# Last group of feed-forward tiles: four tiles with low halves from DVE, evictions first, and a last norm multiplied from PSUM

## The chip, the cores and the metric

The kernel runs on one core of a Trainium2 chip. TensorE (PE) multiplies matrices, VectorE (DVE) and ScalarE (ACT) work on tiles in SBUF and in PSUM, GpSimd (POOL) works on tiles in SBUF and issues some transfers, SyncE (SP) issues the others, and 16 DMA engines move the data. The metric is the time of one execution in microseconds (us); lower is better. The time of a kernel is the median of several runs.

## The reference

One layer of a streaming encoder over 1024 prompt and 64 sample tokens, width 1024, in float32. Three recurrent mixers follow one input projection and are joined by an output projection; then come the feed-forward part and the final norm, which are what matters here:

```python
x = x + jnp.einsum('ble,ed->bld', mix, P['w_out'][l])
xn2 = rmsnorm(x, P['norm_ffn'][l])
hid = (jax.nn.silu(jnp.einsum('bld,df->blf', xn2, P['w_ffn_gate'][l]))
       * jnp.einsum('bld,df->blf', xn2, P['w_ffn_up'][l]))
x = x + jnp.einsum('blf,fd->bld', hid, P['w_ffn_down'][l])
...
y = rmsnorm(x, P['norm_final'])
```

The hidden width is 2816, which is 22 tiles of 128.

## The kernel before

Everything lies transposed: the 128 partitions hold features, the free axis tokens. The tokens form three token groups (`GROUPS`) of 384, 384 and 320. The float32 products are made of three passes in a reduced format (fp32r): each operand is split into a high half (a rounded copy) and a low half (the rest), and `dense` (L128) adds high x high, low input x high weight and, last, high input x low weight in one PSUM tile.

`weights_part` (L110) brings a weight tile of up to four 128 x 128 blocks (256 KB). SP loads it to `raw` (three buffers), ACT casts it to the high half `whi` (L117; five buffers). The low half `wlo` (five buffers) is made in one of two ways. With `add=True`, ACT writes the negated high half (L119) and a DMA that POOL issues reads the weights again and adds them to it (L120). With `add=False`, DVE subtracts the high half from `raw` (L122). A product over five blocks needs two such tiles, one of 128x512 and one of 128x128.

The feed-forward part takes the 22 hidden tiles in five groups (`ffg`, L1292). In each, gate and up products are made for every hidden tile and the three token groups (PSUM tags `pg`, `pu`). Then `down` (L1322) makes the down products: for each of eight output tiles `dm`, a product over the group's hidden tiles into PSUM (`ps_d`, tag `pd`, two buffers), which DVE adds to the residual `x1` (L1326), called the eviction here. In the first four groups a weight tile serves three token groups. In the last one the token groups are the outer loop: 3 x 8 products, each with weights of its own. These 24 products are called the last stage here.

In the last stage each eviction is followed on ACT by a square (L204, L207) and a scaling by the norm's gain (L1338), and on DVE by adding the squares to `sacc` (L210). The final norm of a token group is made while the next one is multiplied: behind the third product (`dm == 2`) PE sums `sacc` over the partitions (`row_sums`, L212, tag `pt`), and DVE computes the inverse root in a chain of small steps and writes two diagonal tiles `dg` (`inv_rms`, L228). Behind the fifth product PE spreads them over the partitions (`spread`, L244), DVE copies the result to SBUF, and `write_y` (L1282) multiplies the eight tiles of `x1` by it and sends them out.

A scheduler sets each engine's order beforehand; an engine works through its list strictly in order. Instructions under `tc.high_priority(offset=WPRIO)` (WPRIO is 400) are taken as if written 400 places earlier; weights and the steps behind the gate and up products have it, the evictions of `down` don't. PE's order is that of the program text (`in_order`, L70).

Of the kernel before, what the change touches and what calls it, by code (L numbers as in the profile page):

```python
# [14 lines left out]
OP = mybir.AluOpType  # L15
# [17 lines left out]
WPRIO = 400  # L33
# [25 lines left out]
def trunk(ctx: ExitStack, tc: tile.TileContext, I: dict, O: list):  # L59
    nc = tc.nc  # L60
    V, A, G, PE = nc.vector, nc.scalar, nc.gpsimd, nc.tensor
    tt = V.tensor_tensor
# [7 lines left out]
    def in_order(ins):  # L70
        if last_pe[0] is not None:
            tc.add_manual_dep(ins, last_pe[0].name, NOSYNC, reason="tensor engine order")
        last_pe[0] = ins

    def mm(out, lhsT, rhs, start=True, stop=True, **kw):
        in_order(PE.matmul(out, lhsT, rhs, start=start, stop=stop, **kw).ins)  # L76
# [48 lines left out]
    def weights(src, add=True):  # L125
        return [p for h0 in range(0, src.shape[1], 4) for p in weights_part(src, h0, add=add)[0]]
# [25 lines left out]
    x1, x2, mhl, sums = {}, {}, {}, {}  # L152
# [91 lines left out]
    def spread(gi, diags, pst, out):  # L244
        T = GROUPS[gi]["T"]
        pn = pst()
        for i, dg in enumerate(diags):
            mm(pn[:, :T], ones_r, dg.rearrange("p i t -> p (i t)")[:, :T], start=(i == 0), stop=(i == 1))
        V.tensor_copy(out[:, :T], pn[:, :T])

    def x2prep(gi, pool, tiles):
        T = GROUPS[gi]["T"]
# [1020 lines left out]
    for i, _ in enumerate(outproj(2, p2, p2, 4, ps_d)):  # L1273
        if i == 1:
            diags = inv_rms(1, row_sums(1, [sums[1]], ps_t))
# [5 lines left out]

    def write_y(gi, diags, out):  # L1282
        T, t0 = GROUPS[gi]["T"], GROUPS[gi]["tok"]
        spread(gi, diags, ps_t, out)
        pieces = (0, 1, 2, 4, 6, 8) if gi == 2 else (0, 2, 4, 6, 8)
        for k0, k1 in zip(pieces, pieces[1:]):
            for k in range(k0, k1):
                xo = x1[gi][:, k, :T]
                (tt if k % 4 != 3 else G.tensor_tensor)(xo, xo, out[:, :T], op=OP.mult)  # L1289
            nc.sync.dma_start(y_out[:, k0:k1, t0:t0 + T], x1[gi][:, k0:k1, :T])  # L1290

    ffg = [4, 4, 4, 5, 5]  # L1292
    f0 = 0
    for fi, nf in enumerate(ffg):
        hid = []
        for m in range(f0, f0 + nf):
# [5 lines left out]
            for gi, grp in enumerate(GROUPS):  # L1302
                T, t0 = grp["T"], grp["tok"]
# [3 lines left out]
                if m == 0 and gi == 0:  # L1307
                    diags = inv_rms(2, row_sums(2, [sums[2]], ps_t))
# [11 lines left out]
        last = fi == len(ffg) - 1  # L1320

        def down(parts, gi, dm):  # L1322
            T, t0 = GROUPS[gi]["T"], GROUPS[gi]["tok"]
            o = ps_d()
            dense(o[:, :T], parts, lambda k: (hid[k][0][:, t0:t0 + T], hid[k][1][:, t0:t0 + T]))
            tt(x1[gi][:, dm, :T], o[:, :T], x1[gi][:, dm, :T], op=OP.add)  # L1326

        for gi in range(3) if last else (None,):
            if last:
                sacc = p2.tile([128, TMAX], F32, tag="sacc", name="sacc", bufs=2)  # L1330
            for dm in range(NK):
                parts = weights(I["w_down"][dm][:, f0:f0 + nf, :])
                for g in (gi,) if last else range(3):
                    down(parts, g, dm)
                if last:
                    xo = x1[gi][:, dm, :GROUPS[gi]["T"]]
                    part = square_sum(sacc, xo, dm, p2, 4, gi == 2 and dm == NK - 1)
                    A.activation(xo, xo, AF.Copy, scale=col("ny", dm))  # L1338
                if dm == 2 and gi:
                    pend = inv_rms(gi - 1, row_sums(gi - 1, [prev], ps_t))  # L1340
                if dm == 4 and gi:
                    write_y(gi - 1, pend, prev)
            prev = sacc if last else None
# [79 lines left out]
```

## Time and profile before

| what | value |
|---|---|
| median of 3 runs | 1402.28 us (1399.97 to 1403.4) |
| profiled execution | 1400.07 us, span 1398.3 us |
| PE busy | 1310.6 us (94%) |
| ACT busy | 651.2 us (47%) |
| DVE busy | 613.5 us (44%) |
| POOL busy | 333.8 us (24%) |
| mean DMA rate | 127 GB/s |

The page of the profile divides the span into 40 equal slices. PE is at 9 tenths (90% or more) from about the 17th to the 37th slice and falls to 8, 8 and 5 in the last three; ACT, POOL and the DMA engines, which have little to do in the middle, rise at the same place. Shares of the whole span say nothing about that end, so the stretches must be read one by one: for each, which engine is busy, what the others wait for, and at which clock PE ran.

### The profile page before, as it was taken

The numbers are of one execution on the slowest core, as the hardware profiler recorded it, in microseconds if no ns is written. First come the engines' busy times: TensorE is split into PE (matmuls) and PEld (weight loads), VectorE is DVE, ScalarE is ACT, GpSimd is POOL, SyncE is SP. The second block draws the span as 40 slices with busy tenths as digits, with TensorE's granted clock in tenths as the row PEclk, the third lists the DMA queues.
The fourth block names the chain that finished last, engine by engine and source line by source line (L and its number), as shares of the span: only waits on it lengthen the run. The fifth ranks groups of instructions, "written<-read, shape, count | busy, mean of one in ns | idle before, by whom it ended". The sixth has DMA issues, their size and how long they took to land.

```text
span 1398.3 us, 21341 instructions
## 1 busy us (share of the span) xinstructions
PE 1310.6 (94%) x7872; PEld 1253.7 (90%) x7872; DVE 613.5 (44%) x1685; ACT 651.2 (47%) x1300; POOL 333.8 (24%) x405
## 2 busy tenths in 40 slices
PE   7878998989988998999999999999999999999885
PEld 7877897878877897999999999999999999999874
DVE  9876798857667577711221121112211121111255
ACT  7766757768875454532213231323132322332763
POOL 2334344434342000110201010101011121111453
PEclk8998999999997999999999999999999999999997
DMA  9967687677692343452525352435344355352996
GB/s 288 290 135 189 130 179 158 152 157 178 137 227 60 115 151 123 108 112 62 122 58 117 65 121 61 102 79 113 69 86 96 63 99 111 75 107 57 174 219 153
DMA packets 114184, 178.22 MB, mean 127 GB/s; under 512 B 13744, under 2 KB 40896, under 8 KB 114080
## 3 DMA queue, kind: packets, MB, share of 16 engines
q0 software_dynamic: 41696, 69.65, 30.8%
q1 hardware_dynamic: 72384, 107.21, 24.3%
q8 instruction: 62, 1.02, 0.3%
q14 instruction: 42, 0.34, 0.1%
HBM read 169.10 MB, written 7.12 MB: 126 GB/s over the span
## 4 chain that ended last, share of the span: by engine, by line
issue 54%; PE 16%; POOL 13%; DVE 10%; DMA 3%; ACT 3%; SPq 0%; POOLq 0%; DVEq 0%; ACTq 0%
POOL wlo L120 12%; PE mm L76 9%; PE mx L76 6%; DMA wlo<-in_w_in_dram 1%; PE pd L76 1%; DMA raw<-in_w_in_dram 1%; ACT wlo L119 0%; DVE x L1289 0%; ACT L138 0%; ACT whi L117 0%; DMA wlo<-in_w_down_dram 0%; DVE xl L325 0%; DVE hist L667 0%; DVE xc L522 0%; SPq L897 0%
## 5 line engine op out<-in xcount | busy, mean ns | idle before, releaser
L117 ACT CAST whi<-raw 128x512 fp32r<-128x512 f32 x336 | 195.2, 585 | 261.0 <-PE pd L76 162.1
L1317 DVE TENSOR_TENSOR sil<-pu,sil 128x384 f32<-128x384 f32 (+1 forms) x66 | 35.3, 536 | 404.5 <-PE pu L76 404.5
L76 PE MATMUL mm<-xh,whi 128*128 128x384 f32 (+1 forms) x480 | 168.4, 358 | 16.8 <-ACT whi L117 8.9
L76 PE MATMUL pd<-hh,whi 128*128 128x384 f32 (+1 forms) x528 | 173.2, 332 | 4.1 <-DVE x L1326 4.1
L76 PE MATMUL pd<-hl,whi 128*128 128x384 f32 (+1 forms) x528 | 172.3, 330 | 0.0
L76 PE MATMUL pg<-x2h,whi 128*128 128x384 f32 (+1 forms) x528 | 170.3, 327 | 0.6 <-ACT x2h L258 0.6
L76 PE MATMUL pg<-x2l,whi 128*128 128x384 f32 (+1 forms) x528 | 170.4, 327 | 0.3 <-DVE x2l L259 0.3
L76 PE MATMUL pu<-x2h,whi 128*128 128x384 f32 (+1 forms) x528 | 170.0, 327 | 0.0
L76 PE MATMUL pu<-x2l,whi 128*128 128x384 f32 (+1 forms) x528 | 169.9, 326 | 0.0
L119 ACT ACTIVATE wlo<-whi 128x512 fp32r<-128x512 f32 (+1 forms) x288 | 164.1, 590 | 4.1 <-issue 1.2
L76 PE MATMUL mm<-xl,whi 128*128 128x384 f32 (+1 forms) x480 | 159.8, 340 | 5.0 <-DVE xl L325 5.0
L120 POOL DMA_DIRECT2D wlo<-in_w_in_dram x112 | 100.2, 980 | 212.6 <-ACT wlo L119 178.9
L120 POOL DMA_DIRECT2D wlo<-in_w_gate_dram x44 | 42.0, 954 | 453.9 <-ACT wlo L119 370.0
L1326 DVE TENSOR_TENSOR x<-pd,x 128x384 f32<-128x384 f32 (+1 forms) x120 | 64.0, 535 | 161.4 <-PE pd L76 161.3
L120 POOL DMA_DIRECT2D wlo<-in_w_down_dram x88 | 77.6, 968 | 216.6 <-ACT wlo L119 175.5
L1318 ACT CAST hh<-sil 128x384 fp32r<-128x384 f32 (+1 forms) x66 | 32.7, 496 | 186.9 <-DVE sil L1317 186.9
L76 PE MATMUL pd<-hh,wlo 128*128 128x384 f32 (+1 forms) x528 | 109.9, 333 | 9.8 <-DMA wlo<-in_w_down_dram 9.7
L76 PEld LDWEIGHTS mm<-xh,whi 128*128 128x128 f32 x480 | 95.2, 199 | 24.5 <-ACT whi L117 9.5
L76 PEld LDWEIGHTS pd<-hh,whi 128*128 128x128 f32 x528 | 100.7, 191 | 4.6 <-ACT whi L117 2.3
L76 PEld LDWEIGHTS pd<-hh,wlo 128*128 128x128 f32 x528 | 90.6, 191 | 14.4 <-DMA wlo<-in_w_down_dram 14.0
L76 PEld LDWEIGHTS mm<-xl,whi 128*128 128x128 f32 x480 | 95.0, 199 | 9.1 <-DVE xl L325 6.3
L76 PE MATMUL mm<-xh,wlo 128*128 128x384 f32 (+1 forms) x480 | 93.4, 333 | 8.4 <-DMA wlo<-in_w_in_dram 8.3
(428 smaller groups left out, 2596.7 us busy)
## 6 DMA issues: line engine op xcount, KB each, us to landing
raw<-in_w_in_dram SPq DMA_DIRECT2D x112, 256.0 KB, 4.5
wlo<-in_w_in_dram POOLq DMA_DIRECT2D x112, 256.0 KB, 5.8
raw<-in_w_down_dram SPq DMA_DIRECT2D x56, 256.0 KB, 4.5
wlo<-in_w_down_dram POOLq DMA_DIRECT2D x56, 256.0 KB, 5.2
raw<-in_w_out_dram SPq DMA_DIRECT2D x48, 256.0 KB, 3.0
raw<-in_w_gate_dram SPq DMA_DIRECT2D x44, 256.0 KB, 2.7
raw<-in_w_up_dram SPq DMA_DIRECT2D x44, 256.0 KB, 5.3
wlo<-in_w_gate_dram POOLq DMA_DIRECT2D x44, 256.0 KB, 4.6
```

The costliest lines, as they stand in the source:

```text
L76: in_order(PE.matmul(out, lhsT, rhs, start=start, stop=stop, **kw).ins)
L117: ins = A.copy(hi[:, :n, :], raw[:, :n, :]).ins
L119: A.activation(lo[:, :n, :], hi[:, :n, :].bitcast(F32), AF.Copy, scale=-1.0)
L120: G.dma_start(lo[:, :n, :], src[:, h0:h0 + n, :], accum_op=OP.add)
L1317: tt(s_[:, :T], pu[:, :T], s_[:, :T], op=OP.mult)
L1318: A.copy(hh[:, t0:t0 + T], s_[:, :T])
L1326: tt(x1[gi][:, dm, :T], o[:, :T], x1[gi][:, dm, :T], op=OP.add)
```

## The change

- The groups of hidden tiles are 5, 5, 4, 4, 4 instead of 4, 4, 4, 5, 5.
- In the last group the low halves of the down weights come from DVE (`add=False`) instead of from an accumulating DMA.
- The evictions of `down`, and the row sums and inverse roots of the first two token groups, have high priority.
- `write_y` makes all eight multiplies of a token group on DVE; two of them were on POOL.
- For the last token group the multiplies read the spread factor from PSUM, without the copy.

```diff
@@ spread
+        if out is None:
+            return pn
         V.tensor_copy(out[:, :T], pn[:, :T])
+        return out
@@ write_y
-        spread(gi, diags, ps_t, out)
+        out = spread(gi, diags, ps_t, None if gi == 2 else out)
...
-                (tt if k % 4 != 3 else G.tensor_tensor)(xo, xo, out[:, :T], op=OP.mult)
+                tt(xo, xo, out[:, :T], op=OP.mult)
...
-    ffg = [4, 4, 4, 5, 5]
+    ffg = [5, 5, 4, 4, 4]
@@ down
-            tt(x1[gi][:, dm, :T], o[:, :T], x1[gi][:, dm, :T], op=OP.add)
+            with tc.high_priority(offset=WPRIO):
+                tt(x1[gi][:, dm, :T], o[:, :T], x1[gi][:, dm, :T], op=OP.add)
@@ loop of the down products
-                parts = weights(I["w_down"][dm][:, f0:f0 + nf, :])
+                parts = weights(I["w_down"][dm][:, f0:f0 + nf, :], not last)
...
-                    pend = inv_rms(gi - 1, row_sums(gi - 1, [prev], ps_t))
+                    with tc.high_priority(offset=WPRIO):
+                        pend = inv_rms(gi - 1, row_sums(gi - 1, [prev], ps_t))
```

The lists of all engines are the same up to the fifth hidden tile of the first group. In the last stage three places of them matter.

ACT, two consecutive products of the first token group, in the kernel before (`whi` are high halves, `wlo` their negation, `sqt` squares, and the last row of a product is the scaling):

```order
L117 CAST whi<-raw 128x128
L117 CAST whi<-raw 128x512
L119 ACTIVATE wlo<-whi 128x128
L119 ACTIVATE wlo<-whi 128x512
L207 ACTIVATE sqt<-x_0_5198 128x384
L1338 ACTIVATE x_0_5198<-x_0_5198,cols 128x384
L117 CAST whi<-raw 128x128
L117 CAST whi<-raw 128x512
L119 ACTIVATE wlo<-whi 128x128
L119 ACTIVATE wlo<-whi 128x512
L207 ACTIVATE sqt<-x_0_5198 128x384
L1338 ACTIVATE x_0_5198<-x_0_5198,cols 128x384
```

and in the changed kernel, three consecutive products:

```order
L117 CAST whi<-raw 128x512
L207 ACTIVATE sqt<-x_0_5198 128x384
L1342 ACTIVATE x_0_5198<-x_0_5198,cols 128x384
L117 CAST whi<-raw 128x512
L207 ACTIVATE sqt<-x_0_5198 128x384
L1342 ACTIVATE x_0_5198<-x_0_5198,cols 128x384
L117 CAST whi<-raw 128x512
L207 ACTIVATE sqt<-x_0_5198 128x384
L1342 ACTIVATE x_0_5198<-x_0_5198,cols 128x384
```

Of the four rows for a product's weights one is left.

DVE, the end of the chain of the first token group's norm, in the kernel before (`x_1<-pd` are the evictions of the 12th and 13th product of the stage, `sc` and `sh` the small steps, `dg` the diagonals, `sacc<-pt` the copy of the spread factor):

```order
L1326 TENSOR_TENSOR x_1_5646<-pd,x_1_5646 128x384
L150 SCALAR_TENSOR_TENSOR sc<-sc 128x3
L232 CAST sh<-sc 128x3
L239 TENSOR_TENSOR dg<-ident,sh 128x384
L237 TENSOR_TENSOR sc<-sc,sh 128x3
L210 TENSOR_TENSOR sacc<-sacc,sqt 128x384
L239 TENSOR_TENSOR dg<-ident,sc 128x384
L215 MEMSET sc 128x9
L1326 TENSOR_TENSOR x_1_5646<-pd,x_1_5646 128x384
L249 COPY sacc<-pt 128x384
```

and in the changed kernel, from the eviction of the 13th product on:

```order
L1330 TENSOR_TENSOR x_1_5646<-pd,x_1_5646 128x384
L148 TENSOR_TENSOR sc<-sc 128x3
L122 TENSOR_TENSOR wlo<-raw,whi 128x512
L149 SCALAR_TENSOR_TENSOR sc<-sc 128x3
L210 TENSOR_TENSOR sacc<-sacc,sqt 128x384
L150 SCALAR_TENSOR_TENSOR sc<-sc 128x3
L232 CAST sh<-sc 128x3
L239 TENSOR_TENSOR dg<-ident,sh 128x384
L237 TENSOR_TENSOR sc<-sc,sh 128x3
L239 TENSOR_TENSOR dg<-ident,sc 128x384
L215 MEMSET sc 128x9
L251 COPY sacc<-pt 128x384
```

The eviction of the 13th product stood behind the second diagonal and now stands nine rows ahead of it, with a low half and a sum of squares in between.

DVE, the norm multiplies of the first token group (`x_0<-x_0,sacc`) in the kernel before, from the copy of the spread factor on:

```order
L249 COPY sacc<-pt 128x384
L210 TENSOR_TENSOR sacc<-sacc,sqt 128x384
L1289 TENSOR_TENSOR x_0_5198<-x_0_5198,sacc 128x384 x6
L1326 TENSOR_TENSOR x_1_5646<-pd,x_1_5646 128x384 x2
L210 TENSOR_TENSOR sacc<-sacc,sqt 128x384 x2
L1326 TENSOR_TENSOR x_1_5646<-pd,x_1_5646 128x384
L210 TENSOR_TENSOR sacc<-sacc,sqt 128x384
```

and in the changed kernel, from the first multiply on:

```order
L1292 TENSOR_TENSOR x_0_5198<-x_0_5198,sacc 128x384 x4
L1330 TENSOR_TENSOR x_1_5646<-pd,x_1_5646 128x384
L122 TENSOR_TENSOR wlo<-raw,whi 128x512
L1292 TENSOR_TENSOR x_0_5198<-x_0_5198,sacc 128x384 x2
L1330 TENSOR_TENSOR x_1_5646<-pd,x_1_5646 128x384
L122 TENSOR_TENSOR wlo<-raw,whi 128x512
L1292 TENSOR_TENSOR x_0_5198<-x_0_5198,sacc 128x384 x2
L1330 TENSOR_TENSOR x_1_5646<-pd,x_1_5646 128x384
L122 TENSOR_TENSOR wlo<-raw,whi 128x512
```

Six multiplies in a row ahead of the next eviction became four, two and two, with an eviction and a low half between them.

## Rows read from the trace of the kernel before

**Rows 1.** stretches; columns: us, busy us (x count) per engine, PEclk, DMA, GB/s.

```profile
590.00:600.00 10.00, 9.03 (x56) 8.59 (x56) 3.29 (x8) 6.53 (x13) 3.48 (x4) 1.00 0.58 120
...
1100.00:1150.00 50.00, 50.00 (x308) 50.00 (x307) 9.64 (x18) 12.93 (x29) 8.95 (x11) 1.00 0.40 78
...
1250.00:1300.00 50.00, 50.00 (x304) 49.90 (x304) 7.49 (x14) 16.06 (x34) 8.49 (x11) 1.00 0.41 82
1300.00:1350.00 50.00, 41.33 (x214) 37.49 (x212) 20.33 (x47) 33.53 (x79) 26.00 (x30) 0.97 0.95 183
1350.00:1399.00 49.00, 28.98 (x157) 26.28 (x157) 26.09 (x69) 21.43 (x51) 18.02 (x19) 0.80 0.74 184
```

**Rows 2.** waits from 1290 to 1399 us; columns: sum us, times, longest us.

```profile
PE pd L76 <- DMA wlo<-in_w_down_dram: 9.7, 12, 1.3
```

**Rows 3.** DMA issues, 430 to 570, then 1290 to 1399 us: size, us landing.

```profile
raw<-in_w_out_dram SPq DMA_DIRECT2D x46, 256.0 KB, 3.0
...
raw<-in_w_down_dram SPq DMA_DIRECT2D x22, 256.0 KB, 4.6
```

**Rows 4.** timeline of PE, last group: start us, us, instruction, idle before, releaser.

```profile
1296.40 0.34 PE L76 MATMUL pd<-hh,whi 128*128 128x384 f32 x1
...
1299.00 0.33 PE L76 MATMUL pd<-hh,whi 128*128 128x384 f32 x1
...
1351.12 0.41 PE L76 MATMUL pd<-hh,whi 128*128 128x384 f32 x1 [2.04 <-DVE x L1326]
...
1374.79 0.31 PE L76 MATMUL pd<-hh,whi 128*128 128x320 f32 x1
...
1376.26 0.90 PE L76 MATMUL pd<-hh,wlo 128*128 128x320 f32 x5
...
1381.74 1.41 PE L76 MATMUL pd<-hh,wlo 128*128 128x320 f32 x5
```

**Rows 5.** timeline of PE, row sums and spread of the first token group.

```profile
1332.60 0.72 PE L76 MATMUL pt<-ones,sacc 128*128 128x1 f32 x6
1333.19 0.42 PE L76 MATMUL pd<-hh,whi 128*128 128x384 f32 x1
...
1341.82 0.62 PE L76 MATMUL pt<-dg,ones_r 128*128 128x384 f32 x1 [0.99 <-DVE dg L239]
1342.24 0.52 PE L76 MATMUL pd<-hh,whi 128*128 128x384 f32 x1
```

**Rows 6.** timeline of DVE, in the chain of that norm.

```profile
1338.83 0.16 DVE L149 SCALAR_TENSOR_TENSOR sc<-sc 128x3 f32<-128x3 f32 x1
1338.91 0.55 DVE L1326 TENSOR_TENSOR x<-pd,x 128x384 f32<-128x384 f32 x1
1339.38 0.16 DVE L150 SCALAR_TENSOR_TENSOR sc<-sc 128x3 f32<-128x3 f32 x1
1339.57 0.17 DVE L232 CAST sh<-sc 128x3 fp32r<-128x3 f32 x1
```

**Rows 7.** groups by shape, whole span; columns: busy us, mean ns, idle before.

```profile
L117 ACT CAST whi<-raw 128x512 fp32r<-128x512 f32 x304 | 186.0, 616 | 225.2 <-PE pd L76 128.3 <-PE mm L76 22.9 <-DMA raw<-in_w_down_dram 20.7
...
L122 DVE TENSOR_TENSOR wlo<-raw,whi 128x512 fp32r<-128x512 f32 x48 | 33.0, 698 | 18.7 <-ACT whi L117 14.4 <-issue 2.4 <-PE mm L76 1.3
...
L1326 DVE TENSOR_TENSOR x<-pd,x 128x320 f32<-128x320 f32 x40 | 19.6, 491 | 51.7 <-PE pd L76 51.7
...
L259 DVE TENSOR_TENSOR x2l<-xT,x2h 128x320 fp32r<-128x320 f32 x8 | 3.5, 483 | 0.0
```

**Rows 8.** one stretch of the last group, after the wait at 1351.12.

```profile
1352.30:1355.10 2.80, 2.80 (x10) 2.80 (x10) 0.56 (x1) 1.70 (x4) 1.49 (x2) 0.50 1.08 306
```

**Rows 9.** timeline of DVE, end of the program.

```profile
1383.19 0.49 DVE L1326 TENSOR_TENSOR x<-pd,x 128x320 f32<-128x320 f32 x1 [2.53 <-PE pd L76]
...
1390.02 0.49 DVE L249 COPY sacc<-pt 128x320 f32<-128x320 f32 x1 [0.73 <-PE pt L76]
1390.55 3.83 DVE L1289 TENSOR_TENSOR x<-x,sacc 128x320 f32<-128x320 f32 x6
```

## Prediction

> **What bounds the kernel now.** I read the busy time by stretch first [rows 1]. TensorE (PE) has no idle time from 1100 to 1150 and from 1250 to 1300 us, at full clock. It is busy only 41.33 of the next 50 us and 28.98 of the last 49. So before 1300 us the price of anything is its matmul time, and only the last feed-forward group can give time back. It starts at 1296.40 and its last product ends at 1381.74 + 1.41 = 1383.15 [rows 4]: 86.75 us.
>
> What the matmuls alone need comes from their spacing. Fifteen 384-wide ones take 1299.00 - 1296.40 = 2.60 us, 0.1733 each; ten 320-wide ones 1376.26 - 1374.79 = 1.47, 0.147 each [rows 4]. The group is 16 products of 384 and 8 of 320, 15 matmuls each: 41.6 + 17.6 = 59.2 us. The other 27.5 us are waiting and half clock. The waits say for what: 12 times for the low halves of the weights [rows 2], and at 1351.12 for a DVE eviction, 2.04 us [rows 4]. Behind the low halves stands the memory traffic: the share of the 16 DMA engines is 0.95 [rows 1], and a 256 KB load lands after 4.6 us [rows 3].
>
> **Fewer tiles in the last group.** Groups of 5, 5, 4, 4, 4 instead of 4, 4, 4, 5, 5 take 3 matmuls out of each of the 24 products: 3 x (16 x 0.1733 + 8 x 0.147) = 11.85 us. They go to a stretch where PE never idles, so this gains nothing by itself: the last group starts at 1296.40 + 11.85 = 1308.25 and its products need 12 matmuls, 2.08 us (384) or 1.76 us (320), 33.3 + 14.1 = 47.4 us in all. What hides the additional weight loads of the two early groups is what hides those of the fourth group now, also of five tiles, whose products run from about 1113 to 1172 us with PE busy all the time [rows 1]. With that cover gone, a product there would wait up to 1.3 us, the longest wait for a low half [rows 2].
>
> **Low halves from DVE.** 48 accumulating DMAs of the last group, their 48 negations on ACT and the 24 small loads go. What is left is 24 loads of 256 KB in some 59 us, 107 GB/s, where 183 were moved [rows 1]. DVE gets 24 subtractions at 0.698 us, and the next instruction starts about 0.08 before an independent one ends [rows 6, 7]: 0.61 each. Per 384-wide product DVE then has the eviction 0.47, the low half 0.61 and the sum of squares 0.47, 1.55 us of the 2.08 that PE needs; per 320-wide one 0.41 + 0.61 + 0.41 = 1.43 of 1.76. ACT has the cast 0.616 [rows 7], a square and a scaling, also below. So the 12 waits for low halves go, in full: five low halves stand ready ahead, and the list of DVE keeps one low half per eviction.
>
> **Evictions and statistics first.** What is late next is the norm of the group before. PE works in program order, and the spread matmuls of the first two token groups stand two products behind the row sums. Between them lies a DVE chain of small steps, 0.19 us apart [rows 6]. The new order puts the evictions into it: the one of the second product (the 13th of the stage) stands before nine of its rows, where in the kernel before it stood behind the last of them. It cannot start before that product is done. After that there remain, with 0.2 us from the end of PE's last slot to the eviction: eviction 0.47, small step 0.08, low half 0.61, small 0.08, sum 0.47, two small 0.38, a diagonal 0.47, small 0.19, the second diagonal 0.55. That is 3.5 us in which PE stands still, where the same spread waited 0.99 us in the kernel before [rows 5]. The second token group's spread waits for 0.2 + 0.41 + 0.57 + 0.08 + 0.41 + 0.47 + 0.19 + 0.55 = 2.9 us by the same reading. Sums cost PE 1333.19 - 1332.60 = 0.59 and the spread after its second diagonal 1342.24 - 1341.82 = 0.42 [rows 5], twice each: 2.0 us. Behind the waiting spread matmul all of PE is queued; DVE itself has little to do then, so nobody else loses.
>
> [...]
>
> The eviction that PE waits 2.04 us for at 1351.12 [rows 4] stands behind six norm multiplies on DVE. In the new order an eviction comes after two to four of them, 0.47 + 0.61 + 2 x 0.47 = 2.0 us per product against 2.08, so that wait goes. In the first four groups raising the evictions is worth nothing, since PE does not wait there.
>
> **The end.** From the last product's end to the span's end are 1398.3 - 1383.15 = 15.15 us. The copy of the spread factor goes: 1390.55 - 1390.02 = 0.53 [rows 9]. The last multiplies now take 3.83 us for six, 0.64 each, while GpSimd does two; all eight on DVE at 0.41, the 0.491 of an eviction less 0.08, take 3.3 + 0.1: 0.45 gained. Two sums of squares now stand behind the last eviction and before the row sums: two dependent adds end 0.45 later than the square that the row sums wait for now. Net 0.5 gained, with bounds of 0 and 1.
>
> The multiplies read PSUM. A 320-wide eviction, which reads PSUM, takes 491 ns and a subtraction of SBUF tiles 483 [rows 7], so reading the factor there costs nothing. [...]
>
> **The sum.** Products 47.4, sums and spreads 2.0, waits 6.4, half clock 2.8: the stage takes 58.6 us and its last product ends at 1308.25 + 58.6 = 1366.85, 16.3 earlier. With the end, 16.8. The profiled execution took 1400.07 us at a span of 1398.3; it would become 1383.3 (span 1381.5). The median of the runs is 2.2 above the profiled one; taken from the median, the time is 1402.28 - 16.8 = 1385.5 us, with 1382 to 1388 for this case.
>
> **Rivals.** *The clock stays.* The same order, but the granted clock stays at 1.00 behind both waits: 2.8 us less, 1382.7. For it speaks that the 12 waits for low halves, up to 1.3 us [rows 2], left the granted clock of that stretch at 0.97 [rows 1]; against it that a wait of 2.04 us did cost clock. 13%.
>
> *The three raw tiles bind.* A raw tile is now free only after DVE's subtraction, so a load is issued when the low half three places ahead is done. Landing 4.6, cast 0.62, low half 0.69 make 5.9 us for three products, 1.97 each: below 2.08, but over the 1.76 of the last eight, 1.7 us. The load of the 22nd tile also stands behind two outputs of 384 KB, 2.5 us at the 306 GB/s of [rows 8]. Together 1.7 to 4.2 us: 1387 to 1390. For it speaks the DMA share; against it that this traffic halves, and that loads of the same size landed in 3.0 us in the output projection [rows 3], where DVE also made the low halves. 15%.
>
> *Slower than before.* The low half stands in DVE's list ahead of the next eviction; if it waits for its load, evictions wait behind it, and with two PSUM buffers PE stops. Time is lost against the kernel before (by more than 0.3%, 4.2 us, about what a measurement of this kernel can tell from no change) once the stage takes 58.6 + 16.8 + 4.2 = 79.6 us, 3.3 per product. That needs three times 3.3 less 1.31, a landing of 8.6 us. Nothing in the trace lands so late. 3%, at 1407 or more.
>
> *The early groups lose what the end gains.* Five tiles in the first group come while its inputs are still made, and PE is not full at 590 us, 9.03 of 10 us [rows 1]. If the ten added weight loads cost 0.2 to 1.3 us each, 2 to 13 us: 1388 to 1399; the last of these is no change. 7%, half of it within 0.3%.
>
> **How the numbers follow.** Forecast 62%, rivals 13, 15, 3 and 7. Forecast, first, second and most of the fourth rival are faster by over 0.3%: 0.93; within it 0.04; slower 0.03. The range takes the first rival with 3 us for the spread between runs below it, 1379, and the second with the same above it, 1394.
>
> **What would show it.** Right, if the profile of the changed kernel shows no PE wait for a low half in the last group, no accumulating DMA there, a DMA share near 0.6, PE waits of 3 to 4 and near 3 us before two spreads and a granted clock of 0.50 behind each. The DVE busy time of the stage should be near 60% and the end about 14.6 us. Wrong, if DVE's low halves wait for loads (second rival), if the two waits are gone, or if PE idles between 600 and 1300 us.

## The result, and the profile after

The changed kernel takes 1386.62 us (median of four runs, 1385.1 to 1388.96); the kernel before, run beside it, takes 1401.12 us (four runs). The ratio is 0.990, with a 95% interval of 0.9876 to 0.9923: 14.5 us faster, where 16.8 were forecast and 1385.5 predicted. The profiled execution of the changed kernel took 1388.96 us at a span of 1387.2.

The stretches that answer to [rows 1] (columns: busy time of each engine with its instructions, then granted clock, DMA share, GB/s):

```profile
core 0: us, PE busy (x) PEld busy (x) DVE busy (x) ACT busy (x) POOL busy (x), PEclk, DMA share, GB/s
1300.00:1350.00 50.00, 47.05 (x271) 46.48 (x270) 31.86 (x70) 27.11 (x49) 0.00 (x0) 0.97 0.36 103
1350.00:1387.00 37.00, 23.05 (x137) 21.29 (x135) 27.54 (x79) 13.89 (x27) 0.00 (x0) 0.80 0.37 125
```

POOL does nothing there any more, the DMA engines are at 0.36 and 0.37 instead of 0.95 and 0.74, and PE is idle for 3 us of the first 50 instead of 9. What PE still waits for is in its list of the last stage (start, duration, and in brackets the wait and who ended it):

```profile
1336.54 0.72 PE L76 MATMUL pt<-ones,sacc 128*128 128x1 f32 x6
1344.26 0.45 PE L76 MATMUL pt<-dg,ones_r 128*128 128x384 f32 x1 [2.73 <-DVE dg L239]
1344.93 0.69 PE L76 MATMUL pt<-dg,ones_r 128*128 128x384 f32 x1 [0.22 <-DVE dg L239]
...
1362.07 0.75 PE L76 MATMUL pd<-hh,wlo 128*128 128x320 f32 x4
1364.93 0.44 PE L76 MATMUL pt<-dg,ones_r 128*128 128x384 f32 x1 [2.11 <-DVE dg L239]
1365.60 0.69 PE L76 MATMUL pt<-dg,ones_r 128*128 128x384 f32 x1 [0.22 <-DVE dg L239]
...
1371.99 0.75 PE L76 MATMUL pd<-hh,wlo 128*128 128x320 f32 x4
1374.41 0.35 PE L76 MATMUL pt<-ones,sacc 128*128 128x1 f32 x2 [1.67 <-DVE sacc L210]
1379.09 1.30 PE L76 MATMUL pt<-dg,ones_r 128*128 128x320 f32 x2 [3.30 <-DVE dg L239]
```

These are all the waits of PE from the stage's first product (1313.66) on. None is for a low half [rows 2] and none for an eviction [rows 4]; two stand before spreads. The stage's last product ends at 1371.99 + 0.75 = 1372.74.

To compare kernels I cut each profiled execution at the same three places: the early part, from the weight load of the first gate product to the first product of the last stage; the stage; and the end, from the stage's last product to the end of the span. The kernel before has 727.0 + 86.75 + 15.15 = 828.9 us, the changed one 738.06 + 59.08 + 14.46 = 811.6: 17.3 less. What comes before the first gate product took 569.4 us before and 575.6 after; to that I come back.

### The profile page after: what moved, and what is told of

Read it like the earlier page. It is cut to its first block, busy times and chain, and to the rows that moved or that the text cites. A ratio compares the mean times of both kernels' runs of the same rounds, so it can differ in the third digit from the quotient of the medians.

```text
span 1387.2 us, 21171 instructions
## 1 busy us (share of the span) xinstructions
PE 1310.5 (94%) x7872; PEld 1257.5 (91%) x7872; DVE 624.1 (45%) x1714; ACT 633.7 (46%) x1244; POOL 293.1 (21%) x359
## 4 chain that ended last, share of the span: by engine, by line
PE 73%; DVE 12%; issue 6%; DMA 4%; ACT 3%; POOL 1%; SPq 0%; DVEq 0%; ACTq 0%; POOLq 0%
PE pd L76 20%; PE pu L76 18%; PE pg L76 18%; PE mm L76 10%; PE mx L76 6%; DMA wlo<-in_w_in_dram 2%; DMA raw<-in_w_in_dram 1%; ACT wlo L119 1%; ACT L138 1%; ACT whi L117 1%; DVE mix L1055 1%; PE pt L76 0%; DMA wlo<-in_w_gate_dram 0%; SPq L900 0%; DVE xl L328 0%
## 5 line engine op out<-in xcount | busy, mean ns | idle before, releaser
L117 ACT CAST whi<-raw 128x512 fp32r<-128x512 f32 x320 | 190.4, 600 | 251.8 <-PE pd L76 176.0
L119 ACT ACTIVATE wlo<-whi 128x512 fp32r<-128x512 f32 x248 | 145.2, 606 | 2.8 <-PE pu L76 0.5
L76 PE MATMUL pd<-hh,wlo 128*128 128x384 f32 (+1 forms) x528 | 106.7, 327 | 0.0
L76 PEld LDWEIGHTS pd<-hl,whi 128*128 128x128 f32 x528 | 100.2, 190 | 0.0
L76 PEld LDWEIGHTS pg<-x2l,whi 128*128 128x128 f32 x528 | 99.1, 188 | 1.0 <-DVE x2l L262 0.7
```

What stands on the lines that cost most here:

```text
L117: ins = A.copy(hi[:, :n, :], raw[:, :n, :]).ins
L119: A.activation(lo[:, :n, :], hi[:, :n, :].bitcast(F32), AF.Copy, scale=-1.0)
```

## The experiments

The table gives the three parts of each profiled execution, their sum, and the ratio of the times to the kernel before in the same comparison.

| kernel | early part | stage | end | sum | median us | ratio, 95% |
|---|---|---|---|---|---|---|
| before | 727.0 | 86.75 | 15.15 | 828.9 | 1401.12 | 1 |
| changed | 738.06 | 59.08 | 14.46 | 811.6 | 1386.62 | 0.9876 to 0.9923 |
| e1_groups | 737.98 | 61.03 | 15.09 | 814.1 | 1385.89 | 0.9877 to 0.9917 |
| e2_lows | 726.78 | 70.41 | 15.11 | 812.3 | 1385.24 | 0.9872 to 0.9913 |
| e3_both | 738.09 | 61.61 | 15.10 | 814.8 | 1387.58 | 0.9889 to 0.9931 |
| d2_small | 725.84 | 78.65 | 15.21 | 819.7 | 1390.31 | 0.9908 to 0.9955 |
| d3_own | 726.59 | 85.05 | 15.26 | 826.9 | 1395.85 | 0.9963 to 0.9998 |
| d1_depth | 738.01 | 68.85 | 15.14 | 822.0 | 1389.37 | 0.9899 to 0.9944 |
| e5_noevict | 739.44 | 63.99 | 13.57 | 817.0 | 1383.71 | 0.9862 to 0.9907 |
| e6_nostat | 739.59 | 61.06 | 14.45 | 815.1 | 1384.55 | 0.9874 to 0.9930 |
| e7_fill | 737.58 | 58.35 | 14.37 | 810.3 | 1383.29 | 0.9863 to 0.9914 |
| e4_late | 738.55 | 56.24 | 15.51 | 810.3 | 1381.94 | 0.9845 to 0.9888 |
| n1_top | 738.15 | 55.62 | 13.63 | 807.4 | 1375.2 | 0.9798 to 0.9846 |
| n2_five | 727.44 | 62.54 | 14.12 | 804.1 | 1372.76 | 0.9780 to 0.9830 |

The median carries what happens before the first gate product as well, which differs by several microseconds between executions (last section). Statements on a part of the change rest on the three parts.

### Which part of the change gives the gain

**e1_groups**, the group sizes alone:

```diff
-    ffg = [4, 4, 4, 5, 5]
+    ffg = [5, 5, 4, 4, 4]
```

> The kernel before with group sizes 5, 5, 4, 4, 4 and nothing else. Theory (the accumulating DMA held the last stage): the stage starts 11.85 us later and stays bound by memory traffic. A product moves 2 x 256 KB instead of 2 x 320 KB, so its 86.75 us shrink at best to 69.4; the gain is 0 to 5.5 us, 1395 to 1401, and PE still waits for low halves. Rival (having fewer tiles there is what gives): the stage falls to about 60 us, the time to about 1386.

Measured: 1385.89 us, a stage of 61.03. The theory on record fell. PE waits for no low half, although all 24 accumulating DMAs of the 128x512 tiles are still there:

```profile
1340.24 0.45 PE L76 MATMUL pt<-dg,ones_r 128*128 128x384 f32 x1 [1.31 <-DVE dg L239]
1341.24 0.44 PE L76 MATMUL pt<-dg,ones_r 128*128 128x384 f32 x1 [0.56 <-DVE dg L239]
1362.08 0.44 PE L76 MATMUL pt<-dg,ones_r 128*128 128x384 f32 x1 [2.75 <-DVE dg L239]
1363.02 0.69 PE L76 MATMUL pt<-dg,ones_r 128*128 128x384 f32 x1 [0.50 <-DVE dg L239]
1369.41 0.39 PE L76 MATMUL pd<-hh,whi 128*128 128x320 f32 x1 [0.96 <-DVE x L1326]
```

These are all its waits in the stage.

**e2_lows**, the low halves alone:

```diff
-                parts = weights(I["w_down"][dm][:, f0:f0 + nf, :])
+                parts = weights(I["w_down"][dm][:, f0:f0 + nf, :], not last)
```

> The kernel before with the low halves of the last group from DVE and nothing else; groups stay 4, 4, 4, 5, 5. Theory (only the way of the low halves counts): matmuls 59.2, sums and spreads 2.0, a spread wait of 1 us and an eviction wait of 2 us for each of two norms with 1.4 us of half clock, so a stage of 68 to 70 us instead of 86.75 and a time of 1382 to 1385, as low as the changed kernel or lower: the new group sizes are needless. Rival (three raw tiles bind): a product of five tiles takes two raw tiles, so three of them are 1.5 products; landing 2.7, cast 0.62 and low half 0.70 make 4.0 us for 1.5 products, 2.7 each against 2.6, and any later landing shows at once: PE waits for weights, stage 72 us or more, time 1388 or more.

Measured: 1385.24 us, a stage of 70.41, no wait for weights. A stage with five tiles has 11.2 us more of products (its early part is that much shorter), so against e1_groups it stands at 70.41 - 11.2 = 59.2 to 61.03. The theory held within 0.5 us of its numbers: one of the two edits is enough, and the two come within 2 us of each other.

**e3_both**, both edits, without priorities and with the old end:

```diff
-    ffg = [4, 4, 4, 5, 5]
+    ffg = [5, 5, 4, 4, 4]
-                parts = weights(I["w_down"][dm][:, f0:f0 + nf, :])
+                parts = weights(I["w_down"][dm][:, f0:f0 + nf, :], not last)
```

> The kernel before with the group sizes 5, 5, 4, 4, 4 and the low halves of the last group from DVE; evictions and statistics at normal priority, the end as before. Theory (the priorities create the two waits before the spreads): spread waits of about 1 us each come back in place of 2.95 and 2.33, and one or two eviction waits of 2 us behind norm multiplies come with them, with up to 1.4 us of half clock behind each; with the 0.5 us that the end gives, 1383 to 1388, within 3 us of the changed kernel. Rival (the priorities are needed): without them evictions stand behind norm work and weights at many places, PE waits over 10 us for them, 1392 or more.

Measured: 1387.58 us, a stage of 61.61. Both edits together are worth no more than either alone. The time is as the theory said, its reason is not: the waits before the spreads are there without any priority. (With five tiles and no priorities, in e2_lows, PE waits 0.79 + 1.16 us before the first spread; here, with four, 3.08 + 0.22.)

```profile
1339.44 0.45 PE L76 MATMUL pt<-dg,ones_r 128*128 128x384 f32 x1 [3.08 <-DVE dg L239]
1347.17 0.41 PE L76 MATMUL pd<-hh,whi 128*128 128x384 f32 x1 [0.85 <-DVE x L1326]
1361.26 0.45 PE L76 MATMUL pt<-dg,ones_r 128*128 128x384 f32 x1 [2.29 <-DVE dg L239]
1368.09 0.39 PE L76 MATMUL pd<-hh,whi 128*128 128x320 f32 x1 [2.21 <-DVE x L1326]
```

### Why fewer tiles help where memory was the limit

Two theories were left: with five tiles a product takes two of the five `whi` and `wlo` buffers, so they reach 2.5 products ahead instead of 5 (A, depth); or the 64 KB transfers of the fifth tile take more from the DMA engines than their bytes (B). Three kernels were to tell them apart; they don't in full, and the question stays open in part.

**d3_own**, the kernel before with buffers of their own for the halves of the small tiles:

```diff
-            hi = wp.tile([128, 4, 128], F32R, tag="whi", name="whi", bufs=WBUF)
-            lo = wp.tile([128, 4, 128], F32R, tag="wlo", name="wlo", bufs=WBUF)
+            if n > 1:
+                hi = wp.tile([128, 4, 128], F32R, tag="whi", name="whi", bufs=WBUF)
+                lo = wp.tile([128, 4, 128], F32R, tag="wlo", name="wlo", bufs=WBUF)
+            else:
+                hi = p2.tile([128, 1, 128], F32R, tag="whi1", name="whi", bufs=4)
+                lo = p2.tile([128, 1, 128], F32R, tag="wlo1", name="wlo", bufs=3)
```

> The kernel before with the same loads and accumulating DMAs, but the high and low halves of the 128x128 tiles in buffers of their own (four and three), so that the five whi and wlo buffers hold 128x512 tiles alone and reach 5 products ahead instead of 2.5. raw keeps its three buffers for both. Theory A (buffer depth of the low halves): the waits for low halves go for the most part, stage 70 to 75 us instead of 86.75, time 1385 to 1390. Theory B (what the transfers take from the DMA engines): DMA share stays at 0.95 or more and the 12 waits stay, stage 82 us or more, time 1396 or more. Both in part: between.

Measured: 1395.85 us, ratio 0.998; the stage falls by 1.7 us only, to 85.05. PE waits for low halves as before, now for those of the small tile:

```profile
1307.81 0.45 PE L76 MATMUL pd<-hh,wlo 128*128 128x384 f32 x1 [2.09 <-DMA wlo<-in_w_down_dram]
...
1326.04 0.44 PE L76 MATMUL pd<-hh,wlo 128*128 128x384 f32 x1 [1.47 <-DMA wlo<-in_w_down_dram]
```

More depth in the halves' buffers alone gives little. The three `raw` buffers stayed shared; more of them were not tried.

**d2_small**, the kernel before with the low half of the 128x128 tile alone from DVE:

```diff
-        return [p for h0 in range(0, src.shape[1], 4) for p in weights_part(src, h0, add=add)[0]]
+        return [p for h0 in range(0, src.shape[1], 4) for p in weights_part(src, h0, add=add or (add is None and h0 == 0))[0]]
...
-                parts = weights(I["w_down"][dm][:, f0:f0 + nf, :])
+                parts = weights(I["w_down"][dm][:, f0:f0 + nf, :], None if last else True)
```

> The kernel before with groups 4, 4, 4, 5, 5; in the last group DVE makes the low half of the 128x128 tiles alone, the 128x512 ones keep the accumulating DMA. Depth of the buffers as before, 64 KB accumulating transfers gone. Theory A (buffer depth): 5.4 us or more of landing against 2.5 products remain, PE still waits for low halves of 128x512 tiles, stage 78 us or more, time 1391 or more. Theory B (the 64 KB accumulating transfers filled the DMA engines): those waits go, stage 70 to 73 us as in e2_lows, time 1385 to 1388.

Measured: 1390.31 us, a stage of 78.65. Seven waits for low halves, 0.41 to 1.89 us and 5.4 us in all, are left. That is what theory A gave (waits for 128x512 tiles, 78 us or more; its time, 1391 or more, was missed by 0.7), and not theory B's 70 to 73. So d3_own speaks against A and d2_small against B: neither explains both.

How far the DMA engines are the limit shows in the time that packets take. Two stretches of ten products, first the kernel before (1300 to 1335 us), then e1_groups (1314 to 1335); q0 is the queue of the accumulating DMAs, q1 that of the loads, and the columns are packets, MB and share of 16 engines:

```profile
q0 software_dynamic: 2795, 3.16, 62.5%
q1 hardware_dynamic: 2879, 3.28, 32.4%
```

```profile
q0 software_dynamic: 1464, 2.67, 74.7%
q1 hardware_dynamic: 1343, 2.43, 32.5%
```

Both queues together, a product takes (62.5 + 32.4)% of 35 us / 10 = 3.3 us of all 16 engines in the kernel before, and (74.7 + 32.5)% of 21 / 10 = 2.25 in e1_groups (107.2%, so packets overlap). PE needs 2.60 and 2.08. By the same reading d2_small takes 2.66 against 2.60 and d3_own 3.30 against 2.60; with low halves from DVE it is 0.99 against 2.08 in the changed kernel (q1 at 47.7% of 25 us, 12 products). So where DMAs make the low halves, the engines take as long per product as PE or longer, and where DVE makes them, less than half.

The fifth tile's own packets are only in part what separates 3.3 from 2.25. Sorted by size, the trace of the kernel before has in this stretch, on q0, 1256 packets of 512 bytes at 0.066 us each on average and 1230 of 2 KB at 0.214; on q1, 1280 at 0.027 and 1279 at 0.112. Those of 512 bytes are the fifth tile's: 117 us of engine time, 0.73 us per product, 22% of the 3.3 for a fifth of the bytes. So theory B is wrong about the small packets: they cost little more than their bytes. Most of the remaining 0.3 us is that packets of 2 KB take less time in e1_groups, 0.190 and 0.091 us. A packet of 512 bytes takes 31% of the time of one of 2 KB on q0 (0.066 of 0.214) and 24% on q1 (0.027 of 0.112). What is dear is the queue of the accumulating DMAs: its packets take 2.4 and 1.9 times as long as those of 512 bytes and 2 KB on q1.

Nor does engine time sort all kernels: e1_groups, 0.17 us per product over PE, has no wait for a low half, d2_small, 0.06 over, has seven. The traces show one more candidate, the three `raw` buffers. A new load goes out when a cast frees one (from 1296 to 1385 us of the kernel before, SP's queue waits 25 times for a cast, 27.7 us in all), and with two loads per product they reach 1.5 products ahead, with one load 3. From 1290 us on, ACT waits for the load ahead of 19 casts in the kernel before and ahead of 3 in e1_groups (columns: sum us, times, longest us):

```profile
ACT whi L117 <- DMA raw<-in_w_down_dram: 22.1, 19, 2.1
```

```profile
ACT whi L117 <- DMA raw<-in_w_down_dram: 2.9, 3, 1.5
```

In d2_small there are 16 such waits and in d3_own 18. Two loads per product in three buffers are not enough to make PE wait: e2_lows has them, and 17 such waits of 11.5 us in all, but its 256 KB loads land in 2.7 us, where the kernel before has 4.6. Late landings are not enough either: e1_groups has 4.9 us. PE waits for weights where both come together. How much each is worth was not shown, since no kernel had more `raw` buffers.

**d1_depth**, e1_groups with the buffers' reach halved by unused tiles:

```diff
+                if last:
+                    with tc.high_priority(offset=WPRIO):
+                        for tag, dt, n in (("raw", F32, 3), ("whi", F32R, WBUF), ("wlo", F32R, WBUF)):
+                            spare = wp.tile([128, 4, 128], dt, tag=tag, name=tag, bufs=n)
+                            A.copy(spare[:, 0, 0:1], eps)
```

> The kernel before with groups 5, 5, 4, 4, 4 (as in e1_groups), but each weight tile of the last stage is followed by an unused tile of each of the tags raw, whi and wlo, so that the same buffers reach only 2.5 products ahead, as with five tiles; the unused tiles get one tiny copy on ACT each and no DMA, three small ACT instructions per product. Theory A (buffer depth made the waits of the kernel before): from a free wlo buffer to a finished low half are 0.62 us of negation and 6.3 us of accumulating DMA, 6.9 us for 2.5 products, 2.8 us each: PE waits for low halves again, the stage is 65 us or more where e1_groups had 61.0, time 1390 or more. Theory B (the 64 KB transfers filled the DMA engines): nothing waits for low halves, stage 60 to 62 us, time about 1386.

Measured: 1389.37 us, a stage of 68.85. The stage is theory A's (65 us or more), but not its mechanism:

```profile
1323.86 0.96 PE L76 MATMUL pd<-hh,wlo 128*128 128x384 f32 x4 [0.33 <-DMA wlo<-in_w_down_dram]
1326.16 0.41 PE L76 MATMUL pd<-hh,whi 128*128 128x384 f32 x1 [1.33 <-ACT x L1343]
...
1344.80 0.66 PE L76 MATMUL pd<-hh,whi 128*128 128x384 f32 x1 [2.63 <-DVE x L1326]
```

One wait for a low half in the whole stage, of 0.33 us. The tiny copies stand on ACT among casts, squares and scalings, and what PE waits for is a scaling on ACT and an eviction. The edit brought a cost of its own, which was not traced further, and the run says nothing on depth.

### What the priorities do

**e5_noevict**, the changed kernel with evictions at normal priority:

```diff
-            with tc.high_priority(offset=WPRIO):
-                tt(x1[gi][:, dm, :T], o[:, :T], x1[gi][:, dm, :T], op=OP.add)
+            tt(x1[gi][:, dm, :T], o[:, :T], x1[gi][:, dm, :T], op=OP.add)
```

> The changed kernel with the evictions of the down products back at normal priority; row sums and inverse roots stay raised. Theory after e3_both (shorter products, not the priorities, put the eviction of the 13th product into the chain; the evictions' priority only keeps multiplies from standing ahead of evictions): the spread waits stay at 2.5 to 3.0 and 2.0 to 2.4 us, and two waits of 1.5 to 2.5 us for evictions behind norm multiplies come back: stage 62 to 64 us, 3 to 5 us slower than the changed kernel. Rival (the evictions' priority makes the spread waits): these fall below 1 us each, stage 57 us or less.

Measured: a stage of 63.99, 4.9 us over the changed kernel's, as the theory had it. The spread waits stay, and an eviction wait is back, one where two were expected:

```profile
1337.23 1.35 PE L76 MATMUL pt<-dg,ones_r 128*128 128x384 f32 x2 [2.73 <-DVE dg L239]
1347.05 0.58 PE L76 MATMUL pd<-hh,whi 128*128 128x384 f32 x1 [1.87 <-DVE x L1329]
1362.22 0.44 PE L76 MATMUL pt<-dg,ones_r 128*128 128x384 f32 x1 [1.82 <-DVE dg L239]
```

Only part of the 4.9 us is waiting. The waits sum to 6.9 us here and 5.3 in the changed kernel, 1.6 more; the rest is clock. The clock is at 0.50 for 13.6 us of this stage and for 6.8 of the changed kernel's. The first wait is 2.73 us in both kernels; here the clock is low until 1343.7 us, 6.5 behind the wait's end, there until 4.0 behind it (columns: PE busy, granted clock, DMA share, GB/s):

```profile
1342.73:1343.23 0.50, 0.50 (x4) 0.50 1.02 372
```

The ratio, 0.9885, is within the changed kernel's interval all the same: the end is 0.9 us shorter, and its part before the first gate product took 567.2 us where the changed kernel's took 575.6. The time alone doesn't show what this priority is worth.

**e6_nostat**, row sums and inverse roots at normal priority:

```diff
-                    with tc.high_priority(offset=WPRIO):
-                        pend = inv_rms(gi - 1, row_sums(gi - 1, [prev], ps_t))
+                    pend = inv_rms(gi - 1, row_sums(gi - 1, [prev], ps_t))
```

> The changed kernel with row sums and inverse roots back at normal priority; the evictions stay raised. Theory: DVE's list is nearly the same, spread waits 2.5 to 3.3 us and 2.0 to 2.6 us, no waits for evictions, stage 58 to 60 us and the time of the changed kernel within 2 us. Rival (the raised statistics shorten the chain): spread waits of over 3.5 us, stage 61 us or more.

Measured: a stage of 61.06, spread waits of 3.08 and 2.52 us, ratio 0.9902 against 0.9900 for the changed kernel. Neither theory's numbers in full: the waits are those of the theory, the stage is 1 us over it. The raised statistics are worth 2 us of stage at most, and about 1.5 of these are clock: it stays low until 6.4 us behind the first wait's end, in the changed kernel until 4.0.

### The waits before the spreads, and the clock

**e4_late**, the changed kernel with row sums one product earlier and spreads one later:

```diff
-                if dm == 2 and gi:
+                if dm == 1 and gi:
-                if dm == 4 and gi:
+                if dm == 5 and gi:
```

> The changed kernel with the row sums of a token group one product earlier (behind the second product) and the spread one product later (behind the sixth). Theory (the two waits before the spreads come from too little distance, and the half clock from the waits): no wait over 0.5 us before either spread, granted clock 1.00 through the stage, stage 59.1 - 2.95 - 2.33 - 2.85 = 51 us, time 1386.6 - 8.1 = 1378.5. Rival (DVE is the bound there): the multiplies of the second norm move behind the last evictions, evictions come late, and the end grows by 2 to 4 us: 1380.5 to 1382.5. Rival on the clock: it falls without a wait, then 1381.3.

Measured: 1381.94 us, a stage of 56.24. Both waits are gone, but a new one stands before the second row sums, whose sums of squares are behind the first norm's multiplies on DVE; the clock is 0.50 behind it, and the end is 1 us longer. The stage fell by 2.8 us where 8.1 were expected; the second theory, DVE as the bound, comes nearest, though at the sums and not at the end.

```profile
1350.67 1.41 PE L76 MATMUL pt<-ones,sacc 128*128 128x1 f32 x6 [3.74 <-DVE sacc L210]
```

**e7_fill**, the changed kernel with matmuls in place of the wait:

```diff
                 if dm == 4 and gi:
+                    dummy = ps2.tile([128, 512], F32, tag="pg", name="pg", bufs=2)
+                    for j in range(14 if gi == 1 else 12):
+                        mm(dummy[:, :384], parts[0][0] , hid[0][0][:, :384], start=True, stop=True)
                     write_y(gi - 1, pend, prev)
```

> The changed kernel with 14 additional matmuls (12 for the second token group) of 384 columns into a PSUM buffer that nobody reads, ahead of the two spreads: 2.4 and 2.1 us of work in place of the wait, which then stands at about 0.5 us. The spreads can't start earlier. Theory (the clock falls because PE stood still): granted clock 1.00 through the stage, stage 59.1 - 2.8 = 56.3 us, time 1383.8. Rival (the clock falls at these places whatever PE does): 0.50 behind the spreads as before, stage 59 us, time as the changed kernel.

Measured: a stage of 58.35. PE never stands still from the stage's start to the first spread, and no clock is lost there: the product behind that spread runs at full clock, its low-half matmuls starting 1.38 us after the product's first.

```profile
1335.10 2.58 PE L76 MATMUL pg<-hh,whi 128*128 128x384 f32 x14
1337.53 0.44 PE L76 MATMUL pt<-dg,ones_r 128*128 128x384 f32 x1
1338.20 0.44 PE L76 MATMUL pt<-dg,ones_r 128*128 128x384 f32 x1 [0.23 <-DVE dg L239]
1338.48 0.34 PE L76 MATMUL pd<-hh,whi 128*128 128x384 f32 x1
...
1339.86 0.85 PE L76 MATMUL pd<-hh,wlo 128*128 128x384 f32 x4
...
1352.01 0.81 PE L76 MATMUL pt<-ones,sacc 128*128 128x1 f32 x6 [1.85 <-DVE sacc L210]
```

The last row is why only 0.7 us came of it. The second row sums stand 44.63 us behind the stage's start (1307.38), in the changed kernel 1358.40 - 1313.66 = 44.74: DVE's sums of squares set that point, not PE, so what was saved at the first spread is waited away there, and the clock falls behind that wait (columns: PE busy, granted clock, DMA share, GB/s):

```profile
1350.00:1352.00 2.00, 0.16 (x2) 1.00 0.00 0
1352.00:1353.00 1.00, 0.99 (x7) 0.83 0.00 0
1353.00:1354.00 1.00, 1.00 (x5) 0.50 0.08 16
```

Behind the second spread, which is filled too, the clock is 1.00 to the end of the stage. So at both spreads the clock fell with the standing still and not without it. The reverse doesn't hold: not every standing still brought it down (last section).

### A version that beats both

**n1_top**, spreads one product later, sums of squares raised like the evictions, statistics raised above them:

```diff
-                    part = square_sum(sacc, xo, dm, p2, 4, gi == 2 and dm == NK - 1)
+                    with tc.high_priority(offset=WPRIO):
+                        part = square_sum(sacc, xo, dm, p2, 4, gi == 2 and dm == NK - 1)
...
-                    with tc.high_priority(offset=WPRIO):
+                    with tc.high_priority(offset=2 * WPRIO):
                         pend = inv_rms(gi - 1, row_sums(gi - 1, [prev], ps_t))
-                if dm == 4 and gi:
+                if dm == 5 and gi:
```

> The changed kernel with the spread of the first two norms behind the sixth product instead of the fifth, the sums of squares at the evictions' priority, and row sums and inverse roots at twice that. Theory (the waits before the spreads come from too little distance and from evictions in the chain): about 1.2 us of wait before the first spread, under 0.5 us before the second, stage 59.1 - 1.8 - 2.0 = 55.3 us with the clock falling, 52.5 without, time 1380 to 1383, the end up to 1 us longer because multiplies of the second norm stand near it. Rival: the row sums of the second norm wait for sums of squares behind multiplies, as the 3.74 us of e4_late: stage 57 us or more.

Measured: 1375.2 us, a stage of 55.62. Waits before the first spread of 0.66 and 0.56 us (1.2 expected) cost no clock; 1.65 and 0.50 before the second (under 0.5 expected) did. The time is 5 us below the range expected, and the end 0.8 us shorter than the changed kernel's where up to 1 us more was expected.

**n2_five**, the same with the old group sizes:

```diff
-    ffg = [5, 5, 4, 4, 4]
+    ffg = [4, 4, 4, 5, 5]
```

> The same as n1_top with groups 4, 4, 4, 5, 5: products of the last stage take 2.6 and 2.2 us, so DVE and the loads have more room per product. Theory (once the low halves come from DVE, the length of a product only matters as cover for DVE): no wait over 0.5 us before the spreads or for evictions, stage 59.2 + 2.0 + 0 to 2 = 61 to 63 us, time 1377 to 1380. Rival (fewer tiles are needed): PE waits for raw or high halves, stage 66 us or more, time over 1383.

Measured: 1372.76 us, ratio 0.9805, 4 us below the range expected. The stage is as expected, 62.54 us, 3.3 more than its matmuls' 59.2, and PE waits 0.24 us in it:

```profile
1300.00:1350.00 50.00, 50.00 (x308) 50.00 (x307) 42.05 (x115) 34.94 (x76) 0.00 (x0) 1.00 0.51 151
1350.00:1357.00 7.00, 6.35 (x39) 5.46 (x37) 6.49 (x15) 3.62 (x9) 0.00 (x0) 1.00 0.27 79
```

(The columns are those of the first rows under the result.) PE is busy all 50 us at full clock. By the three parts it is 7.5 us better than the changed kernel and 3.3 better than n1_top: with low halves from DVE five tiles are the better choice for the last group, which fits the waits that are gone: a product of 2.60 us is more cover for what DVE does in one. (The ratios of the two kernels, 0.9822 and 0.9805, don't tell them apart.) The time is about 1% below the changed kernel's by the two ratios, more than 7.5 us; in the profiled executions the rest lies before the first gate product, where the engines' lists are the same.

## Why the prediction was right, and which steps were wrong

**Right in sum.** The three parts fell by 17.3 us, where 16.8 were forecast: the stage 59.08 us (58.6), the early part 11.06 longer (11.85), the end 0.69 shorter (0.5). The median fell by 14.5 us against the 1401.12 of the kernel before in the same comparison; the 2.3 us that are missing lie within the spread of its executions (1395.81 to 1403.4). The profiled execution took 1388.96 us where 1383.3 was forecast for one like that of before; 575.6 - 569.4 = 6.2 us of it stand before the first gate product.

**Fewer tiles: the step that failed.** "So this gains nothing by itself" holds for the matmuls and not for the stage. Alone the group sizes took the stage from 86.75 to 61.03 us and gained the whole 1%. I priced the moved matmuls and gave all waits for low halves to the other edit. But the fifth tile brings two transfers of its own per product, 0.73 us of all DMA engines, and takes a second of three `raw` buffers; without it the low halves come in time. Which of the two counts for how much stays open. That the sum came out right is luck in this step: the other edit removes the same waits a second time.

**Low halves from DVE.** The 12 waits went in full, as forecast. But the two edits share one gain: by the three parts the low halves alone gain 16.6 us (828.9 - 812.3), the group sizes alone 14.8, both together 14.1 (e3_both).

**Evictions and statistics first.** The lengths were right. From the end of PE's last slot before the first spread (1341.37) to the second diagonal's matmul (1344.93) are 3.56 us (3.5), at the second spread 1365.60 - 1362.66 = 2.94 (2.9). DVE's list shows the working of the sum, from the eviction of the 13th product on:

```profile
1341.57 0.56 DVE L1330 TENSOR_TENSOR x<-pd,x 128x384 f32<-128x384 f32 x1
...
1342.11 0.68 DVE L122 TENSOR_TENSOR wlo<-raw,whi 128x512 fp32r<-128x512 f32 x1
...
1342.79 0.55 DVE L210 TENSOR_TENSOR sacc<-sacc,sqt 128x384 f32<-128x384 f32 x1
...
1343.65 0.56 DVE L239 TENSOR_TENSOR dg<-ident,sh 128x384 fp32r<-128x384 f32 x1
...
1344.31 0.56 DVE L239 TENSOR_TENSOR dg<-ident,sc 128x384 fp32r<-128x384 f32 x1
```

The cause was wrong. I put it down to the raised evictions; e3_both and e5_noevict have the same waits without them. The chain takes some 7.5 us from row sums to diagonals (in the changed kernel from 1337.13 to the first diagonal's matmul at 1344.26 and the second's at 1344.93), and a product got 0.52 us shorter, two of them 1.04; from e2_lows to e3_both, where only the group sizes differ, the first spread's waits grow from 1.95 to 3.30 us. What raising the evictions does is to keep multiplies from standing ahead of them. That is 4.9 us of stage from e5_noevict to the changed kernel, of which 1.6 are waits and the rest clock; from e3_both, which lacks the other small edits too, it is 2.5.

**The clock.** Right in kind and size. Behind the first wait PE ran from 1345 to 1348.5 at 0.50, as in [rows 8] (columns as in the first rows under the result):

```profile
1345.00:1346.00 1.00, 1.00 (x3) 1.00 (x4) 0.36 (x2) 0.00 (x0) 0.00 (x0) 0.50 0.01 4
1346.00:1348.00 2.00, 2.00 (x8) 2.00 (x8) 1.97 (x5) 0.00 (x0) 0.00 (x0) 0.50 0.00 0
1348.00:1349.00 1.00, 1.00 (x7) 1.00 (x6) 0.21 (x1) 0.62 (x1) 0.00 (x0) 0.86 0.79 278
```

From 1344.93 to the low-half matmuls two products on (1350.20) are 5.27 us, where full clock needs 0.28 (that spread in e7_fill) + 2.08 + 1.39 = 3.75: 1.52 lost, and 1.41 at the second wait by the same count. The 2.8 us of half clock in the sum, 1.4 for each wait, were an estimate: half of the 2.80 us for which PE ran at 0.50 behind the wait of 2.04 us in the kernel before [rows 4, 8]. No run shows the 2.8 itself; the changed kernel shows 2.93 in its place. e7_fill shows that without the standing still the clock stays. The size has some luck in it: behind a wait of the same 2.73 us e5_noevict lost more. The reading of the kernel before had also missed that its first spread, behind waits of 0.51 and 0.99 us, already brought the clock down: its next matmul took 0.52 us [rows 5] where those at full clock took 0.34 [rows 4], and the granted clock is 0.50 from 1341.9 to 1345.3 us. So the 0.42 us taken for a spread is a half-clock figure, 0.28 at full clock.

**The end.** 0.69 gained, 0.5 forecast. The eight multiplies from PSUM take 0.41 us each, as forecast, where six on DVE took 0.64 each [rows 9]; the copy ahead of them is gone:

```profile
1373.19 1.08 DVE L210 TENSOR_TENSOR sacc<-sacc,sqt 128x320 f32<-128x320 f32 x2
...
1380.43 3.27 DVE L1292 TENSOR_TENSOR x<-x,pt 128x320 f32<-128x320 f32 x8 [0.73 <-PE pt L76]
```

Reading the factor from PSUM does not show as a cost: the multiplies of the first norm in the same trace, which read an SBUF copy, are no faster for their width, 0.49 us each at 384 columns against 0.41 at 320:

```profile
1346.25 1.97 DVE L1292 TENSOR_TENSOR x<-x,sacc 128x384 f32<-128x384 f32 x4
```

**The rivals.** The three raw tiles did not bind: loads landed in 2.6 us (median of 12 from 1315 to 1340 us) instead of the 4.6 taken [rows 3], with 134 GB/s moved in that stretch, where the kernel before moved 183 [rows 1]. The early groups lost nothing: PE has no wait between 600 and 1313 us. (The fourth group's products, taken from 1113 to 1172 us in the kernel before, ran there from 1118.7 to 1178.0, with PE busy all the time.) The clock did not stay. Two signs were off in size: DVE is busy for 48.3 of the stage's 59.1 us, 82% and not near 60, and the DMA share there is 0.41 and not near 0.6.

## What to carry to other kernels

When two edits attack the same wait, try each alone: here either one gave the whole gain, and a third choice, the old group sizes with the new low halves, was the best base. Price a transfer by the engine time of its packets and not by its bytes alone (a packet of 2 KB took 0.21 us in an accumulating DMA, 0.11 in a plain one), and set that, and the number of buffers that it lands in, against PE's time per product. A step that PE waits for in program order must stand as many products behind its source as its chain takes, counted anew whenever products get shorter.

## What was not expected of the hardware

The clock does not fall behind every wait. Waits of 2.5 us or more within the last stage (2.52 to 3.74 us, in the changed kernel, e1_groups, e3_both, e4_late, e5_noevict, e6_nostat, d1_depth, d2_small and d3_own) each had PE at 0.50 behind them. The low clock lasted 3.4 us where it began after the wait; where it had begun during the wait, it lasted until 6.0 to 6.5 us behind the wait's end. Of shorter waits some brought the clock down (0.51 and 0.99 us before the first spread of the kernel before, 2.04 at 1351.12 there [rows 4], 2.11 in the changed kernel, 1.85 in e7_fill), some not: e2_lows kept 1.00 behind all six of its waits of 0.79 to 1.55 us, e3_both behind 2.29 us and behind 2.21 us before the last product. In d1_depth a wait of 2.21 us at that place did bring the clock down. What decides between them was not tried, and differences of one or two microseconds between stages can come from it.

The part ahead of the first gate product took 562.8 to 575.6 us in the fourteen profiled executions, though every engine's list is the same there in all of these kernels. That is more than most of the edits are worth. Where it comes from was not tried; it is why parts of one execution are compared here, and medians only for what is larger.
